# Setting one PSUM bank of the mixer apart, feeding transposes a pair earlier at the layer boundaries, and pumping the adaLN vectors at 1.25 in the first FFN

## The chip, the cores and the metric

The kernel runs on one core of a Trainium2 chip. Its time is the device time of one execution in microseconds; the change is judged by that time. The core's engines have a queue each: PE (matmul), DVE and ACT (elementwise work), POOL, and SP, which here issues most DMAs. An engine takes its instructions in order, so an instruction that waits holds up all behind it on that engine. [...]

## The reference, cut to what matters

One layer on 256 tokens of width 2048, in float32: a first FFN, a mixer, a second FFN, each with a layer norm whose shift, scale and gate come from a vector c (adaLN), and a scaled residual.

```python
mod = silu(c) @ w_ada + b_ada              # 9 vectors of 2048: shift, scale, gate for each of 3 parts
x = ln(ALPHA * x + gate0 * swiglu(modulate(x, ...), ffn1_w_in, ffn1_w_out))     # D_FF = 5632
m = modulate(x, ...) @ w_in                # queries, keys, values and gates of the mixer
#   8 softmax heads of width 128 with a forget-gate bias on the logits,
#   4 mLSTM heads (keys 128, values 256) behind a causal convolution of width 4
x = ln(ALPHA * x + gate1 * (concat(fox, mlstm) @ w_out))
x = ln(ALPHA * x + gate2 * swiglu(modulate(x, ...), ffn2_w_in, ffn2_w_out))
```

An mLSTM head forms, over all 256 tokens at once, a matrix of decays from its gates times the scores k.q, multiplies it with the values, and divides by a normaliser.

## The kernel before

**Products.** Every weight is streamed once from memory in pieces of 1 MB (`raw_...`, three buffers, issued on SP). A piece is split into a rounded part `hi` on ACT (L142) and the rest `lo` on DVE (L143), and each product is three matmuls: hi*hi (L369), lo*hi (L370), hi*lo (L371), in `mm3`. The tokens sit in PE's weight side or its moving side, with outputs of 128x256 or 128x512. Stages follow each other in time: first FFN in (tiles `s`, `gu_f`), its out projection (`o_f`), boundary 1, the mixer's input products (`mo`, `fv`, `mv`, `m0`, `m1`, `fb`, `fbk`, `fa`, `fak`, `b_fv`), its out projection (`o_mx`), boundary 2, second FFN.

**The adaLN queue.** The 9 vectors are not matmuls: DVE accumulates 128x1024 pieces of `w_ada` (`ar`, two buffers, 512 KB each) with `acc = ar * csil[k] + acc` (L157), 16 pieces per accumulator. Then `acc` is split into `ahi` and `alo`, PE sums over partitions with a matmul against ones (`bc`, L170), and DVE takes the diagonal of it (`dg` L188, reduce L190) or adds it to the gate (L211). All this is one generator; a stage calls `pump(rate)` after each of its weight pieces, which adds the rate to what is owed and runs that many accumulations. A `PAUSE` inside the generator ends a pump early, so that matmuls lie between the split, the sum and the diagonal. The rates stand in one line (`R_F, R_IN, R_OUT, R_MX, R_A, R_B`). `need(n)` runs the queue on until n parts are done, where the next stage uses them.

**PSUM.** Five banks (tag `mm`, `mm_tile`) rotate for the accumulating products, three (tag `aux`, `aux_tile`) for all else: transposes `tp`, `bc`, and in the mixer an mLSTM head's gate sums `gb`, scores `sps` and outputs `nps`. A tile of a tag takes the bank of the tile that many allocations before it and waits for that one's last reader.

**mLSTM heads.** `mlstm_head(o, h)` puts its gate sum (L1225) and scores (L1227) on PE, ACT turns the gate sum into decays (L1230, L1231), DVE masks them (L1232) and multiplies them with the scores (`dm`, L1233), PE forms `nps` (L1239, L1241), DVE the normaliser `dn`, ACT scales (L1248) and squares in place (L1249). The heads are side steps, taken between the weight pieces of `fb`, `fbk` and `fa`. The scores have two tiles: `sps` for 256 queries, and a corner of `gb`. The softmax heads' queries and keys (`pr_fb`, `pr_fbk`, `pr_fa`, `pr_fak`) are two tiles each, from `form_a_four`, read by ACT (L1307, L1312).

**Boundary.** `boundary` normalises 256 tokens, modulates and transposes them. For each pair of 128 columns and each half of the tokens, ACT forms `n` (L312), PE transposes it (`tp`, L316), DVE or ACT applies shift and scale (`xf`, L323 and L326), then `xhi_mx` (L332) and `xlo_mx` (L334) are split off. DVE's order (and ACT's, in the first part) is written out by hand with `next()` on the generators of `modulate_tile`; the first weight pieces' products run between. Boundary 1 has 8 such pairs, boundary 2 has 4. Elsewhere a scheduler sets each engine's order ahead of the run.

Of the kernel before, what the change touches and what calls it, by code (L numbers as in the profile page):

```python
# [14 lines left out]
P = 128  # L15
T = 256
# [16 lines left out]
def layer_kernel(  # L33
# [24 lines left out]
    wp.tile([P, 1024], F32R, tag="lo", bufs=6, name="lo_place")  # L58
    ap = ctx.enter_context(tc.tile_pool(name="ap", bufs=1))
    sm = ctx.enter_context(tc.tile_pool(name="sm", bufs=2))  # L60
    pm = ctx.enter_context(tc.tile_pool(name="pm", bufs=5, space=PSUM))
    pa = ctx.enter_context(tc.tile_pool(name="pa", bufs=3, space=PSUM))

    def mm_tile(name):
        return pm.tile([P, 512], F32, tag="mm", name=name)

    def aux_tile(name):
        return pa.tile([P, 512], F32, tag="aux", name=name)
# [204 lines left out]
    def ntag():  # L273
        seq[0] += 1
        return str(seq[0])
# [29 lines left out]
    def modulate_tile(v, a, k0, nk, rs, xT, xs=None, on_v=False):  # L305
        ts_ = slice(a * P, (a + 1) * P)
        n = npool.tile([P, nk * P], F32, tag="n", bufs=2, name=f"n_{ntag()}")
        r = res[:, a, k0 * P:(k0 + nk) * P]
        if on_v:
            V.tensor_scalar(out=n, in0=r, scalar1=rs[:, 2:3], scalar2=rs[:, 0:1], op0=ALU.add, op1=ALU.mult)  # L310
        else:
            S.activation(n, r, AF.Identity, bias=rs[:, 1:2], scale=rs[:, 0:1])  # L312
        tp = aux_tile(f"tp{ntag()}")
        tpv = tp.rearrange("p (k t) -> p k t", k=4)
        for q in range(nk):
            PE.transpose(tpv[:, q, :], n[:, q * P:(q + 1) * P], ident)  # L316
        yield
        xf = npool.tile([P, nk, P], F32, tag="xf" if xs is None else "xe", bufs=2 if xs is None else 6,
                        name=f"xf{ntag()}")
        for q in range(nk):  # L320
            k = k0 + q
            if q % 2 and (a or k0 >= 6):
                V.tensor_scalar(out=xf[:, q, :], in0=tpv[:, q, :], scalar1=scsh[:, v + 1, k:k + 1],  # L323
                                scalar2=scsh[:, v, k:k + 1], op0=ALU.mult, op1=ALU.add)
            else:
                S.activation(xf[:, q, :], tpv[:, q, :], AF.Identity,  # L326
                             bias=scsh[:, v, k:k + 1], scale=scsh[:, v + 1, k:k + 1])
            if xs is not None:
                xs[a, k] = xf[:, q, :]
        yield  # L330
        hi, lo = (x[:, k0:k0 + nk, ts_] for x in xT)
        S.copy(hi, xf)  # L332
        yield
        yield V.tensor_tensor(out=lo, in0=xf, in1=hi.bitcast(F32), op=ALU.subtract)  # L334
# [195 lines left out]
    def boundary(add_up, st, lgb, v, tag, xT, entry, nk, raws):  # L530
        mv, rs, sums, mr = ([small(n, t, f"{t}_{tag}{a}") for a in range(2)]
                            for n, t in ((2, "mv"), (1, "rs"), (10, "sums"), (3, "mr")))
        xs = {}
        ws = []
        sq = mm_tile(f"sq_{tag}")

        def w_hi():
            k = len(ws)
            hi = wp.tile([P, 1024], F32R, tag="hi", bufs=6, name=f"hi_{tag}e{k}")
            S.copy(hi, raws[k // 2][:, k % 2, :])  # L540
            ws.append((k, hi, wp.tile([P, 1024], F32R, tag="lo", bufs=6, name=f"lo_{tag}e{k}")))

        def w_lo(k):
            V.tensor_tensor(out=ws[k][2], in0=raws[k // 2][:, k % 2, :], in1=ws[k][1].bitcast(F32), op=ALU.subtract)

        dve, act = mybir.EngineType.DVE, mybir.EngineType.Activation
        m = [[modulate_tile(v, a, k, 2, mr[a], xT, xs if k < 6 else None, a + k == 0) for k in range(0, nk, 2)]
             for a in range(2)]
        m0, m1 = m
        with tc.manual_schedule(engines={dve, act}):  # L550
            for _ in add_up(0):
                pass
            together(row_std(mv[0], rs[0], st[0]))
            aff = [ln_affine(a, rs[a], mv[a], lgb, sums[a], sq) for a in range(2)]
            lns = [ln_stats(mr[a], sums[a]) for a in range(2)]
            w_hi()
            for _ in aff[0]:
                pass
            together(lns[0])
            up = add_up(1)  # L560
            together(lns[0])
            w_hi()
            next(m0[0])
            together(lns[0])
            next(m0[1])
# [24 lines left out]
            next(m1[1])  # L590
            next(m1[0])
            w_lo(1)
            next(m1[1])
            next(m1[0])
            next(m1[1])
            next(m1[0])
            w_lo(2)
            next(m1[1])
            w_lo(3)
        with tc.manual_schedule(engines={dve}):  # L600
            for i in range(3, len(m0)):
                for _ in range(2):
                    for b in (m0[i], m1[i]):
                        next(b)
                if i == 3:
                    next(m1[2])
                    for b in (m0[2], m1[2]):
                        next(b)
                for b in (m0[i], m1[i]):
                    next(entry, None)  # L610
                    next(b)
                    last = next(b)
        return last, mr, xs, ws
# [61 lines left out]

    R_F, R_IN, R_OUT, R_MX, R_A, R_B = 1.25, 1.2, 1, 1.42, 1.05, .6
    NP = 2
    right = dict(side="right")  # L680
    def at(rate):
# [314 lines left out]
    emptied = [None]  # L996


    def cols_form_b(c0, col, ws, use, name):
        ps = {(a, b): mm_tile(f"b_{name}{col}{a}{b}") for b in range(len(ws)) for a in range(2)}  # L1000
        cb = [sum(ws[:b]) for b in range(len(ws) + 1)]
        for u in range(4):
            for k4, hi, lo in load_w(W[u * 512:(u + 1) * 512, c0 + col:c0 + col + cb[-1]], 4, cb[-1],
# [29 lines left out]


    def form_a_four(c0, name, before_last=lambda: None):
        ps = [mm_tile(f"pr_{name}{i}") for i in range(2)]
        for u in range(4):
            if u == 3:
                before_last()
# [177 lines left out]
    def mlstm_head(o, h):  # L1217
# [2 lines left out]
            yield True  # L1220
        qm, km = o[:, 0, :], o[:, 1, :]
        gb = aux_tile(f"gb{h}")
        sps = [aux_tile(f"sps{h}")[:, :T], gb[:, T:T + P]]
        dm = mx.tile([P, T + P], F32, tag="dm", bufs=2, name=f"dm{h}")
        PE.matmul(gb[:, :T], sel(h), ng, start=True, stop=True)  # L1225
        for i in range(2):
# [103 lines left out]
    fox_heads(4, "b", lambda h: [f"o{h - 4}"])  # L1330
    side += [mlstm_out(h) for h in range(NMH)]
    fox_heads(0, "a", lambda h: [f"qs{h + 4}"])
    cols_form_b(C_FV, 0, [512], use_fv, "fv")
    done.add("fv0")
    xp.release()

# [175 lines left out]
```

## Time and profile before

| | |
|---|---|
| median of 3 runs | 1930.44 us (1929.65 to 1933.3) |
| profiled execution | 1936.89 us, of which the profile's span is 1935.1 |
| granted TensorE clock, mean | 0.994 |
| PE busy | 1892.8 us, 98% |
| DVE, ACT busy | 1486.0 us (77%), 952.6 us (49%) |
| DMA | 510.90 MB, mean 264 GB/s |

Where PE is busy nearly all the time, the time is its busy time plus its gaps; a row of waits names the engine and instruction that ended a gap. In timelines the bracket behind an instruction is the idle time just before it and its releaser. A clock below 1.00 stretches every matmul in that stretch.

### The profile page before, as it was taken

To read this page: it belongs to the slowest core of one execution; us is meant where nothing else is said; L and a number is where in the kernel's file an instruction comes from. 1 tells how busy PE (TensorE), PEld (TensorE's weight loads), DVE (VectorE), ACT (ScalarE), POOL (GpSimd) and SP (SyncE) were. 2 spreads that over 40 slices of the span, in tenths; PEclk is the share of its full clock that TensorE was granted. 3 is DMA by queue.
4 is the path that set the end of the run, shared out by engine and by line. 5 is a ranking of instruction groups with operands and counts; after the bars stand their busy time and mean duration, and the time that the engine had idled before them with its cause. 6 is when DMAs were issued, how large, how long until landed. Compare 5 with 4: busy or idle time off the path is not lost.

```text
span 1935.1 us, 32288 instructions
## 1 busy us (share of the span) xinstructions
PE 1892.8 (98%) x13085; PEld 1722.3 (89%) x13085; DVE 1486.0 (77%) x1838; ACT 952.6 (49%) x1359; POOL 56.4 (3%) x82
## 2 busy tenths in 40 slices
PE   6999999999999999999989999999999999999997
PEld 3999999999988887699989876999999999988886
DVE  6788988777788998888887888767766665555776
ACT  3554454443454554845755635555444444444552
POOL 1111100000000000100000000000000000000000
PEclk9999999999999999999999999999999999999998
DMA  9978969999898886498887895987776776755552
GB/s 354 377 260 315 326 224 302 308 313 320 292 331 289 287 303 218 154 326 295 300 290 237 301 301 167 314 298 240 253 254 225 262 237 196 238 187 187 194 196 87
DMA packets 283421, 510.90 MB, mean 264 GB/s; under 512 B 10850, under 2 KB 134146, under 8 KB 282248
## 3 DMA queue, kind: packets, MB, share of 16 engines
q1 hardware_dynamic: 275496, 480.53, 73.4%
q0 software_dynamic: 7776, 28.32, 4.2%
q8 instruction: 102, 1.67, 0.4%
q14 instruction: 47, 0.39, 0.1%
HBM read 506.71 MB, written 2.10 MB: 263 GB/s over the span
## 4 chain that ended last, share of the span: by engine, by line
PE 73%; issue 12%; DMA 7%; DVE 6%; ACT 1%; POOL 0%; SPq 0%; DVEq 0%; POOLq 0%; ACTq 0%
PE gu_f L370 8%; PE gu_f L371 8%; PE gu_f L369 8%; PE o_f L369 7%; PE o_f L371 7%; PE o_f L370 7%; DMA ar<-in_w_ada_dram 5%; PE s L369 5%; PE s L370 5%; PE s L371 5%; DVE acc L157 2%; PE fh L369 2%; PE fh L371 2%; PE fh L370 1%; PE fs L371 1%
## 5 line engine op out<-in xcount | busy, mean ns | idle before, releaser
L157 DVE SCALAR_TENSOR_TENSOR acc<-ar,csil,acc 128x1024 f32<-128x1024 f32 x242 | 307.7, 1272 | 91.6 <-DMA ar<-in_w_ada_dram 89.7
L370 PE MATMUL s<-xlo_f,hi_s 128*128 128x256 f32 x768 | 213.5, 278 | 1.8 <-DVE xlo_f L300 1.8
L369 PE MATMUL s<-xhi_f,hi_s 128*128 128x256 f32 x768 | 213.4, 279 | 0.0
L371 PE MATMUL s<-xhi_f,lo_s 128*128 128x256 f32 x768 | 213.2, 278 | 0.0
L371 PE MATMUL gu_f<-xhi_f,lo_f2i 128*128 128x256 f32 x768 | 212.0, 276 | 0.0
L369 PE MATMUL gu_f<-xhi_f,hi_f2i 128*128 128x256 f32 x768 | 212.0, 276 | 0.0
L370 PE MATMUL gu_f<-xlo_f,hi_f2i 128*128 128x256 f32 x768 | 212.0, 276 | 0.0
L143 DVE TENSOR_TENSOR lo_f2i<-raw_f2i,hi_f2i 128x1024 fp32r<-128x1024 f32 x96 | 117.6, 1225 | 89.0 <-ACT hi_f2i L142 89.0
L371 PE MATMUL gu_f<-xhi_f,lo_f1i 128*128 128x256 f32 x640 | 176.7, 276 | 0.0
L369 PE MATMUL gu_f<-xhi_f,hi_f1i 128*128 128x256 f32 x640 | 176.7, 276 | 0.0
L370 PE MATMUL gu_f<-xlo_f,hi_f1i 128*128 128x256 f32 x640 | 176.7, 276 | 0.0
L142 ACT CAST hi_f2i<-raw_f2i 128x1024 fp32r<-128x1024 f32 x96 | 100.7, 1049 | 135.2 <-PE gu_f L370 122.4
L142 ACT CAST hi_s<-raw_s 128x1024 fp32r<-128x1024 f32 x96 | 100.6, 1051 | 130.4 <-PE s L370 90.5
L370 PEld LDWEIGHTS s<-xlo_f,hi_s 128*128 128x128 f32 x768 | 145.3, 189 | 2.1 <-DVE xlo_f L300 2.1
L371 PEld LDWEIGHTS s<-xhi_f,lo_s 128*128 128x128 f32 x768 | 145.3, 189 | 0.0
L369 PEld LDWEIGHTS s<-xhi_f,hi_s 128*128 128x128 f32 x768 | 144.8, 189 | 0.2 <-ACT hT1b L827 0.2
L369 PEld LDWEIGHTS gu_f<-xhi_f,hi_f2i 128*128 128x128 f32 x768 | 144.2, 188 | 0.2
L370 PEld LDWEIGHTS gu_f<-xlo_f,hi_f2i 128*128 128x128 f32 x768 | 144.2, 188 | 0.2
L371 PEld LDWEIGHTS gu_f<-xhi_f,lo_f2i 128*128 128x128 f32 x768 | 144.2, 188 | 0.0
L143 DVE TENSOR_TENSOR lo_f2o<-raw_f2o,hi_f2o 128x1024 fp32r<-128x1024 f32 x88 | 107.7, 1224 | 44.9 <-ACT hi_f2o L142 44.8
L143 DVE TENSOR_TENSOR lo_s<-raw_s,hi_s 128x1024 fp32r<-128x1024 f32 x96 | 115.8, 1220 | 30.5 <-ACT hi_s L142 29.6
L369 PE MATMUL o_f<-hi_f2o,hh 128*128 128x512 f32 x344 | 135.2, 393 | 0.0
(449 smaller groups left out, 5377.1 us busy)
## 6 DMA issues: line engine op xcount, KB each, us to landing
ar<-in_w_ada_dram SPq DMA_DIRECT2D x227, 512.0 KB, 5.4
raw_f2i<-in_ffn_w_in_dram SPq DMA_DIRECT2D x48, 1024.0 KB, 5.2
raw_s<-in_ffn_w_in_dram SPq DMA_DIRECT2D x47, 1024.0 KB, 7.7
raw_f1o<-in_ffn_w_out_dram SPq DMA_DIRECT2D x44, 1024.0 KB, 7.5
raw_f2o<-in_ffn_w_out_dram SPq DMA_DIRECT2D x44, 1024.0 KB, 5.1
raw_f1i<-in_ffn_w_in_dram SPq DMA_DIRECT2D x40, 1024.0 KB, 6.9
ar<-in_w_ada_dram POOLq DMA_DIRECT2D x48, 512.0 KB, 6.9
raw_mxo<-in_w_out_dram SPq DMA_DIRECT2D x16, 1024.0 KB, 7.7
```

The costliest lines, as they stand in the source:

```text
L142: S.copy(hi, src)
L143: return V.tensor_tensor(out=lo, in0=src, in1=hi.bitcast(F32), op=ALU.subtract)
L157: V.scalar_tensor_tensor(out=acc, in0=raw, scalar=csil[:, k:k + 1], in1=acc, op0=ALU.mult, op1=ALU.add)
L369: PE.matmul(o, ah, bh, start=start, stop=False)
L370: PE.matmul(o, ah, bl, start=False, stop=False)
L371: PE.matmul(o, al, bh, start=False, stop=stop)
```

## The change

Three things. The five rotating banks become four with tag `mm` and one with tag `m5`; `mm_tile` counts turns and gives every fifth tile to `m5`, so that outside the mixer the turn is as before. In the mixer `form_a_four` and the last `cols_form_b` take only the four (`four=True`), and the fifth holds the scores `sps` of the mLSTM heads, which leave the three auxiliary banks. At the boundaries `columns(i + 1)` (the `n`, transposes and `xf` of the next pair) is called ahead of the lower parts of pair i, and the buffers of `xf` are 4 and 4 instead of 2 and 6. In the first FFN's input the rate goes from 1.2 to 1.25 accumulations per weight piece, of which 40 pump.

```diff
@@ -58,11 +58,19 @@
     wp.tile([P, 1024], F32R, tag="lo", bufs=6, name="lo_place")
     ap = ctx.enter_context(tc.tile_pool(name="ap", bufs=1))
     sm = ctx.enter_context(tc.tile_pool(name="sm", bufs=2))
-    pm = ctx.enter_context(tc.tile_pool(name="pm", bufs=5, space=PSUM))
+    pm = ctx.enter_context(tc.tile_pool(name="pm", bufs=1, space=PSUM))
     pa = ctx.enter_context(tc.tile_pool(name="pa", bufs=3, space=PSUM))
 
-    def mm_tile(name):
-        return pm.tile([P, 512], F32, tag="mm", name=name)
+    turn = [0]
+
+    def fifth_tile(name):
+        return pm.tile([P, 512], F32, tag="m5", name=name)
+
+    def mm_tile(name, four=False):
+        turn[0] = 0 if four else turn[0] % 5 + 1
+        if turn[0] == 5:
+            return fifth_tile(name)
+        return pm.tile([P, 512], F32, tag="mm", bufs=4, name=name)
 
     def aux_tile(name):
         return pa.tile([P, 512], F32, tag="aux", name=name)
@@ -315,8 +323,7 @@
         for q in range(nk):
             PE.transpose(tpv[:, q, :], n[:, q * P:(q + 1) * P], ident)
         yield
-        xf = npool.tile([P, nk, P], F32, tag="xf" if xs is None else "xe", bufs=2 if xs is None else 6,
-                        name=f"xf{ntag()}")
+        xf = npool.tile([P, nk, P], F32, tag="xf" if xs is None else "xe", bufs=4, name=f"xf{ntag()}")
         for q in range(nk):
             k = k0 + q
             if q % 2 and (a or k0 >= 6):
@@ -544,8 +551,8 @@
             V.tensor_tensor(out=ws[k][2], in0=raws[k // 2][:, k % 2, :], in1=ws[k][1].bitcast(F32), op=ALU.subtract)
 
         dve, act = mybir.EngineType.DVE, mybir.EngineType.Activation
-        m = [[modulate_tile(v, a, k, 2, mr[a], xT, xs if k < 6 else None, a + k == 0) for k in range(0, nk, 2)]
-             for a in range(2)]
+        m = [[modulate_tile(v, a, k, 2, mr[a], xT, xs if 4 * a <= k < 6 else None, a + k == 0)
+              for k in range(0, nk, 2)] for a in range(2)]
         m0, m1 = m
         with tc.manual_schedule(engines={dve, act}):
             for _ in add_up(0):
@@ -598,14 +605,19 @@
             next(m1[1])
             w_lo(3)
         with tc.manual_schedule(engines={dve}):
-            for i in range(3, len(m0)):
+            def columns(i):
                 for _ in range(2):
                     for b in (m0[i], m1[i]):
                         next(b)
+
+            columns(3)
+            for i in range(3, len(m0)):
                 if i == 3:
                     next(m1[2])
                     for b in (m0[2], m1[2]):
                         next(b)
+                if i + 1 < len(m0):
+                    columns(i + 1)
                 for b in (m0[i], m1[i]):
                     next(entry, None)
                     next(b)
@@ -675,7 +687,7 @@
 
 
 
-    R_F, R_IN, R_OUT, R_MX, R_A, R_B = 1.25, 1.2, 1, 1.42, 1.05, .6
+    R_F, R_IN, R_OUT, R_MX, R_A, R_B = 1.25, 1.25, 1, 1.42, 1.05, .6
     NP = 2
     right = dict(side="right")
     def at(rate):
@@ -996,8 +1008,8 @@
     emptied = [None]
 
 
-    def cols_form_b(c0, col, ws, use, name):
-        ps = {(a, b): mm_tile(f"b_{name}{col}{a}{b}") for b in range(len(ws)) for a in range(2)}
+    def cols_form_b(c0, col, ws, use, name, four=False):
+        ps = {(a, b): mm_tile(f"b_{name}{col}{a}{b}", four) for b in range(len(ws)) for a in range(2)}
         cb = [sum(ws[:b]) for b in range(len(ws) + 1)]
         for u in range(4):
             for k4, hi, lo in load_w(W[u * 512:(u + 1) * 512, c0 + col:c0 + col + cb[-1]], 4, cb[-1],
@@ -1033,7 +1045,7 @@
 
 
     def form_a_four(c0, name, before_last=lambda: None):
-        ps = [mm_tile(f"pr_{name}{i}") for i in range(2)]
+        ps = [mm_tile(f"pr_{name}{i}", True) for i in range(2)]
         for u in range(4):
             if u == 3:
                 before_last()
@@ -1220,7 +1232,7 @@
             yield True
         qm, km = o[:, 0, :], o[:, 1, :]
         gb = aux_tile(f"gb{h}")
-        sps = [aux_tile(f"sps{h}")[:, :T], gb[:, T:T + P]]
+        sps = [fifth_tile(f"sps{h}")[:, :T], gb[:, T:T + P]]
         dm = mx.tile([P, T + P], F32, tag="dm", bufs=2, name=f"dm{h}")
         PE.matmul(gb[:, :T], sel(h), ng, start=True, stop=True)
         for i in range(2):
@@ -1330,7 +1342,7 @@
     fox_heads(4, "b", lambda h: [f"o{h - 4}"])
     side += [mlstm_out(h) for h in range(NMH)]
     fox_heads(0, "a", lambda h: [f"qs{h + 4}"])
-    cols_form_b(C_FV, 0, [512], use_fv, "fv")
+    cols_form_b(C_FV, 0, [512], use_fv, "fv", True)
     done.add("fv0")
     xp.release()
```

The number of instructions of each engine stays the same; their order changes. Line numbers after the change are larger by 7 to 12.

PE, in the mixer, around mLSTM head 2 (`nps_10508` is head 0's second output, `gb_10524` and `sps_10525` head 2's gate sum and scores), before:

```order
L1239 MATMUL nps_10508<-yM_8718,dm_10332 128x257
L1241 MATMUL nps_10508<-yM_8718,dm_10332 128x257
L1225 MATMUL gb_10524<-ng,rowsel 128x256
L1227 MATMUL gb_10524<-o_9834 128x128
L369 MATMUL pr_fbk_10444<-xhi_mx,hi_fbk_10540 128x256
L370 MATMUL pr_fbk_10444<-xlo_mx,hi_fbk_10540 128x256
...
L1227 MATMUL sps_10525<-o_9834 128x256
```

The same place after (`nps_10523`, `gb_10539`, `sps_10540`):

```order
L1251 MATMUL nps_10523<-yM_8733,dm_10372 128x257
L1253 MATMUL nps_10523<-yM_8733,dm_10372 128x257
L1237 MATMUL gb_10539<-ng,rowsel 128x256
L1239 MATMUL sps_10540<-o_9847 128x256
L1239 MATMUL gb_10539<-o_9847 128x128
L376 MATMUL pr_fbk_10459<-xhi_mx,hi_fbk_10555 128x256
```

The scores move from 22 rows behind the gate sum to the row next to it.

DVE, in the mixer, up to the multiplication of head 0's decays with its scores (`dm_10332`), before:

```order
L143 TENSOR_TENSOR lo_fbk_10541<-raw_fbk_10538,hi_fbk_10540 128x1024
L157 SCALAR_TENSOR_TENSOR acc_0_10402<-ar_0_2_10409,csil,acc_0_10402 128x1024
L188 TENSOR_TENSOR dg_1_1_10316<-bc_1_1_10313,ident 128x512
L157 SCALAR_TENSOR_TENSOR acc_0_10402<-ar_0_3_10412,csil,acc_0_10402 128x1024
L190 TENSOR_REDUCE scsh<-dg_1_1_10316 128x4
L1232 TENSOR_TENSOR dm_10332<-dm_10332,trir 128x128
L192 TENSOR_TENSOR scsh<-scsh,bcol 128x2x4
L1232 TENSOR_TENSOR dm_10332<-dm_10332,trir 128x128
L1233 TENSOR_TENSOR dm_10332<-sps_10331,dm_10332 128x256
L1233 TENSOR_TENSOR dm_10332<-gb_10330,dm_10332 128x128
```

DVE after, from the same multiplication (`dm_10372`) to that of head 1 (`dm_10447`, whose last part reads `gb_10445`):

```order
L1245 TENSOR_TENSOR dm_10372<-sps_10371,dm_10372 128x256
L165 SCALAR_TENSOR_TENSOR acc_0_10120<-ar_0_10_10285,csil,acc_0_10120 128x1024
L1245 TENSOR_TENSOR dm_10372<-gb_10370,dm_10372 128x128
L151 TENSOR_TENSOR lo_fbk_10638<-raw_fbk_10635,hi_fbk_10637 128x1024
L151 TENSOR_TENSOR lo_fbk_10666<-raw_fbk_10635,hi_fbk_10665 128x1024
L165 SCALAR_TENSOR_TENSOR acc_0_10120<-ar_0_11_10354,csil,acc_0_10120 128x1024
L1244 TENSOR_TENSOR dm_10447<-dm_10447,trir 128x128
L165 SCALAR_TENSOR_TENSOR acc_0_10120<-ar_0_12_10357,csil,acc_0_10120 128x1024
L1245 TENSOR_TENSOR dm_10447<-sps_10446,dm_10447 128x256
L1244 TENSOR_TENSOR dm_10447<-dm_10447,trir 128x128
L151 TENSOR_TENSOR lo_fbk_10736<-raw_fbk_10733,hi_fbk_10735 128x1024
L1245 TENSOR_TENSOR dm_10447<-gb_10445,dm_10447 128x128
```

The diagonal of `bc_1_1` and its reduce no longer stand ahead of head 0's masks; three lo products and two accumulations stand between head 0's last part and that of head 1.

DVE, in the mixer's out projection, at the last accumulations of part 2 (`ar_2_14`, `ar_2_15`), before:

```order
L438 SCALAR_TENSOR_TENSOR res<-res,o_mx_11741 128x512
L143 TENSOR_TENSOR lo_mxo_30_12319<-raw_mxo_3_12316,hi_mxo_30_12318 128x1024
L157 SCALAR_TENSOR_TENSOR acc_2_12026<-ar_2_14_12257,csil,acc_2_12026 128x1024
L441 BN_STATS st_mx_11737<-res 128x6
L157 SCALAR_TENSOR_TENSOR acc_2_12026<-ar_2_15_12296,csil,acc_2_12026 128x1024
L143 TENSOR_TENSOR lo_mxo_31_12323<-raw_mxo_3_12316,hi_mxo_31_12322 128x1024
L436 TENSOR_TENSOR o_mx_12138<-o_mx_12138,gate 128x512
L143 TENSOR_TENSOR lo_mxo_10_12331<-raw_mxo_1_12328,hi_mxo_10_12330 128x1024
```

And after:

```order
L448 BN_STATS st_mx_11752<-res 128x6
L165 SCALAR_TENSOR_TENSOR acc_2_11906<-ar_2_15_12150,csil,acc_2_11906 128x1024
L445 SCALAR_TENSOR_TENSOR res<-res,o_mx_11755 128x512
L151 TENSOR_TENSOR lo_mxo_10_12234<-raw_mxo_1_12231,hi_mxo_10_12233 128x1024
L151 TENSOR_TENSOR alo_2_0_12192<-acc_2_11906,ahi_2_0_12191 128x512
...
L445 SCALAR_TENSOR_TENSOR res<-res,o_mx_11757 128x512
L151 TENSOR_TENSOR lo_mxo_30_12333<-raw_mxo_3_12330,hi_mxo_30_12332 128x1024
L448 BN_STATS st_mx_11753<-res 128x6
L151 TENSOR_TENSOR lo_mxo_31_12337<-raw_mxo_3_12330,hi_mxo_31_12336 128x1024
L196 TENSOR_TENSOR dg_2_0_12270<-bc_2_0_12267,ident 128x512
```

The last accumulation, `ar_2_15`, moves from two rows ahead of the add-up of the second 1024 columns to the add-up of the first; the first half of its split (`alo_2_0`) and its diagonal (`dg_2_0`) stand among the lo products instead.

## The prediction

> **What bounds the kernel now.** I read the page first, then the waits of PE, then busy time by stage, and last the timeline around each wait.
>
> ```profile
> span 1935.1 us, 32288 instructions
> ...
> PE 1892.8 (98%) x13085; PEld 1722.3 (89%) x13085; DVE 1486.0 (77%) x1838; ACT 952.6 (49%) x1359; POOL 56.4 (3%) x82
> ```
> ```profile
> PE sps L1227 <- DVE dm L1233: 5.8, 2, 4.4
> ...
> PE o_mx L370 <- DVE lo_mxo L143: 1.8, 2, 1.1
> PE bc L170 <- DVE alo L143: 1.4, 1, 1.4
> ...
> PE o_mx L369 <- DVE res L438: 1.1, 1, 1.1
> PE tp L316 <- DVE xf L323: 0.7, 1, 0.7
> ...
> PE o_mx L369 <- ACT yF L1054: 0.5, 1, 0.5
> ...
> PE nps L1239 <- DVE dm L1233: 0.2, 1, 0.2
> PE sps L1227 <- ACT nps L1249: 0.2, 1, 0.2
> ```
>
> PE is busy 98% of the span, and neither the number of its instructions nor that of any other engine changes. So the change can only win or lose what PE waits. These rows (us in total, times, longest) are all of PE's waits that lie in stages the change touches: 5.8 + 1.8 + 1.4 + 1.1 + 0.7 + 0.5 + 0.2 + 0.2 = 11.7 us. The next fence has busy time by stage (length, then PE, PEld, DVE, ACT, POOL, the granted PE clock, DMA share, GB/s).
>
> ```profile
> 276.00:516.00 240.00, 240.00 (x2107) 239.48 (x2105) 192.94 (x206) 104.10 (x126) 0.56 (x1) 1.00 0.92 307
> ...
> 1210.00:1500.00 290.00, 289.92 (x2414) 283.55 (x2413) 209.67 (x245) 144.86 (x206) 0.00 (x0) 1.00 0.80 264
> 1500.00:1780.00 280.00, 280.00 (x2026) 261.83 (x2025) 162.94 (x160) 124.93 (x145) 0.00 (x0) 1.00 0.67 219
> ```
> ```profile
> 983.00:987.00 4.00, 0.07 (x1) 0.00 (x0) 3.38 (x11) 0.56 (x2) 0.00 (x0) 0.90 0.84 270
> 987.00:993.00 6.00, 5.54 (x24) 5.39 (x25) 4.33 (x5) 2.50 (x7) 0.00 (x0) 0.50 1.00 346
> 993.00:1000.00 7.00, 7.00 (x57) 6.83 (x57) 5.36 (x10) 3.70 (x8) 0.00 (x0) 1.00 0.58 193
> ```
>
> In the first FFN's input stage (276 to 516) and in the whole second FFN PE never stands still: a faster pump there earns nothing by itself. The last three rows show a cost that the list of waits leaves out. PE stood still from 983 to 987; then 24 matmuls took 6.00 us at clock 0.50, where 57 took 7.00 us at clock 1.00, so 24 would take 2.95: 3.05 us more. The mixer's heads thus cost 5.8 + 0.2 + 0.2 + 3.05 = 9.2 us.
>
> **Heads (fifth bank).** Rows of PE, ACT and DVE around heads 1 and 2 (start, duration, engine, line; idle time and its releaser in brackets):
>
> ```profile
> 972.11 0.70 PE L1227 MATMUL sps<-o 128*128 128x256 f32 x2 [1.36 <-DVE dm L1233]
> 979.94 0.48 PE L1225 MATMUL gb<-ng,rowsel 128*128 128x256 f32 x1
> 987.46 1.19 PE L1227 MATMUL sps<-o 128*128 128x256 f32 x2 [4.39 <-DVE dm L1233]
> ```
> ```profile
> 975.72 1.05 ACT L142 CAST hi_fbk<-raw_fbk 128x1024 fp32r<-128x1024 f32 x1 [1.15 <-PE pr_fbk L370]
> 987.17 0.39 ACT L1249 ACTIVATE nps<-yM 128x256 f32<-128x256 f32 x1
> ```
> ```profile
> 968.64 0.68 DVE L188 TENSOR_TENSOR dg<-bc,ident 128x512 f32<-128x512 f32 x1
> ...
> 971.97 0.28 DVE L1233 TENSOR_TENSOR dm<-gb,dm 128x128 f32<-128x128 f32 x1
> ...
> 979.21 1.22 DVE L143 TENSOR_TENSOR lo_fbk<-raw_fbk,hi_fbk 128x1024 fp32r<-128x1024 f32 x1
> ...
> 981.88 1.28 DVE L157 SCALAR_TENSOR_TENSOR acc<-ar,csil,acc 128x1024 f32<-128x1024 f32 x1 [1.45 <-DMA ar<-in_w_ada_dram]
> ```
>
> `sps2` at 987.46 is put down to DVE's `dm`, but no `dm` ends there on DVE. What ends at 987.46 is ACT's square of `nps00` (987.17): `sps2` takes the auxiliary bank that `nps00` holds. With a bank of its own `sps2` no longer waits for it: 4.39 goes, and 0.19 at `sps3`. `sps1` now waits for head 0's `dm<-sps`, on the same DVE as before, but the order after has `dg` and its reduce (I take 0.6 us each, the row's 0.68 less the overlap of neighbours) no longer ahead of it: 1.36 shrinks to about 0.2.
>
> What is late next? The auxiliary banks now turn gb0, gb1, nps00, nps01, gb2: `gb2` takes `gb1`'s bank and waits for DVE's `dm<-gb1`, which the order puts behind three lo products and two accumulations. `gb2` would be due at 979.94 - 1.4 = 978.5. On DVE head 0's `dm` ends near 971.1, one accumulation and its last part by 972.4, a lo product by 973.6; the next lo needs the cast of 975.72, which PE releases 1.2 us earlier, so it runs from 975.6 to 976.8; two accumulations (2.4), the masks and `dm<-sps1` (0.8), one lo product (1.15) and `dm<-gb1` (0.28) end at 981.4. `gb2` waits 2.9 us (0 if the scheduler's order is met, 4.5 if one accumulation finds its row as late as at 981.88). With 0.3 for later squares the heads keep 0.2 + 2.9 + 0.3 = 3.4, and gain 5.8, provided that the clock stays up. A wait of 1.36 kept it; in the row of 983 to 987 the mean of 0.90 over 4 us means 0.8 us at half clock, so it fell about 3.1 us into the wait. 2.9 is just below, and I take the full clock; the half clock would give 3.05 back.
>
> [...]
>
> **Boundaries.** In boundary 1 the n, transposes and `xf` of pair i+1 now stand ahead of hi/lo of pair i; boundary 2 has four pairs and one turn of that loop, so nothing moves there.
>
> ```profile
> 803.67 0.44 PE L316 MATMUL tp<-ident,n 128*128 128x128 f32 x2 [0.73 <-DVE xf L323]
> ```
> ```profile
> 798.60 1.05 ACT L142 CAST hi_mo<-raw_mo 128x1024 fp32r<-128x1024 f32 x1 [1.48 <-DMA raw_mo<-in_w_in_dram]
> 801.96 0.59 ACT L312 ACTIVATE n<-res,mr 128x256 f32<-128x256 f32 x1
> ```
>
> The transposes that waited 0.73 move seven matmuls earlier on PE, but their `n` still stands on ACT behind two casts, the first of which waits 1.48 for its weights; `n` ends at about 802.1 and PE arrives at about 801.1. The stall changes its place and its releaser: 0, between -0.7 (the whole stall) and +1.
>
> **R_IN and the queue behind it.** 40 pumps at 1.25 make 50 accumulations in the first FFN's input instead of 48. They hide: the row of 276 to 516 has DVE free for 47 us and DMA for 8%, that is 19 us, and two accumulations take 2.5 us of DVE. From there the queue runs 2 to 8 accumulations ahead, so other pieces of it meet the places where PE waits.
>
> ```profile
> 755.16 0.50 PE L170 MATMUL bc<-ahi,trir 128*128 128x512 f32 x1
> 760.04 0.50 PE L170 MATMUL bc<-alo,trir 128*128 128x512 f32 x1 [1.40 <-DVE alo L143]
> ```
> ```profile
> 759.30 0.68 DVE L143 TENSOR_TENSOR alo<-acc,ahi 128x512 fp32r<-128x512 f32 x1
> ```
>
> Here the order after has `alo` six lo products of 1.15 us earlier on DVE, done near 753, and PE takes both halves together where it took the first, near 755: -1.4 (0 if DVE ran 2 us late).
>
> ```profile
> 1088.33 1.21 DVE L143 TENSOR_TENSOR lo_mxo<-raw_mxo,hi_mxo 128x1024 fp32r<-128x1024 f32 x1
> ...
> 1120.26 2.60 DVE L157 SCALAR_TENSOR_TENSOR acc<-ar,csil,acc 128x1024 f32<-128x1024 f32 x2 [1.85 <-DMA ar<-in_w_ada_dram]
> ...
> 1127.67 1.28 DVE L157 SCALAR_TENSOR_TENSOR acc<-ar,csil,acc 128x1024 f32<-128x1024 f32 x1 [1.94 <-DMA ar<-in_w_ada_dram]
> ...
> 1134.78 1.28 DVE L157 SCALAR_TENSOR_TENSOR acc<-ar,csil,acc 128x1024 f32<-128x1024 f32 x1 [1.76 <-DMA ar<-in_w_ada_dram]
> ...
> 1139.45 1.29 DVE L436 TENSOR_TENSOR o_mx<-o_mx,gate 128x512 f32<-128x512 f32 x2
> ...
> 1164.29 1.28 DVE L157 SCALAR_TENSOR_TENSOR acc<-ar,csil,acc 128x1024 f32<-128x1024 f32 x1 [1.35 <-DMA ar<-in_w_ada_dram]
> ```
> ```profile
> 1168.55 0.50 PE L370 MATMUL o_mx<-lo_mxo,yh 128*128 128x512 f32 x1 [1.07 <-DVE lo_mxo L143]
> ```
>
> In the mixer's out projection the last accumulations of part 2, with the wait of 1.35 at 1164.29, stood just ahead of the lo products that PE waited for (1.07 of them at 1168.55). After, the last one is before them by ten rows; two `alo`, a `dg` and a reduce of 0.6 each come instead. The waits list's 1.8 us go (0 to 2.3). The price is paid earlier: between the lo product at 1088.33 and the first add-up at 1139.45 stand 16 accumulations instead of 12. With two row buffers they come in pairs every 7.1 to 7.4 us (1120.26, 1127.67, 1134.78), 3.6 us each: 14 beyond the two already loaded take 50 us, which is about the stretch's own length (51). So the wait of 1.1 at the first add-up stays and grows by an estimated 1.0 (-1.1 to +5). At the stage's start DVE has fewer accumulations before the softmax, ACT's copy of `b_fv` comes earlier and the 0.5 goes (+1.4 if the four-bank turn makes another tile wait for the same copies).
>
> **The four-bank turn.** Only `pr_fa1` gets a bank that may still be read: `pr_fb1`'s, which ACT reads last for head 7.
>
> ```profile
> 1008.50 0.28 PE L369 MATMUL pr_fa<-xhi_mx,hi_fa 128*128 128x256 f32 x1
> ```
> ```profile
> 1003.78 0.38 ACT L1307 ACTIVATE qs<-pr_fb 128x256 f32<-128x256 f32 x1
> ```
>
> 4.3 us lie between; ACT's order after puts a scaling and a square (1 us) ahead of that read: hidden, 0, with 3.3 us to spare. If they are used up, the wait is what is left over. [...]
>
> **Sum.** -5.8 (heads) - 1.4 (`bc`) + 0 (boundary) - 0.5 + 1.0 - 1.8 (out projection) = -8.5 us. The profiled execution took 1936.89 (1935.1 of span, 1.8 around it), 6.5 above the median; none of the terms hangs on that difference, so it is carried over: 1928.4 against that execution, 1930.44 - 8.5 = 1921.9 against the median.
>
> **The rivals.**
> - Half clock after `gb2`: DVE is slightly later than worked out, the wait passes 3.1 us. For: DVE's accumulations there waited 1.45 for rows. Price 3.05: 1925.0. Chance 0.20.
> - The wait only moves: `gb2` takes over all but about 2.5 of the heads' 9.2, and the out projection's tail is paid back at the first add-up (+1.8): 1930.44 - 2.5 - 1.4 + 1.3 = 1927.8. Chance 0.10.
> - Every wait goes: 9.2 + 1.4 + 0.7 + 0.5 + 1.1 + 1.8 = 14.7, 1915.7. Against: `dm<-gb1` stands late in the order. Chance 0.08.
> - Four banks are too few: if ACT's reads came 8 us later than now, `pr_fa1` would wait 8 - 3.3 = 4.7 us, and an `o_mx` tile the 1.4 + 0.5 worked out above: 1921.9 + 6.6 = 1928.5. It decides from 3.3 us of lateness. Against: the 4.3 us at `pr_fa1`, and ACT's share of 49%. Chance 0.05.
> - Slower: the out projection starves. The 16 accumulations wait for rows on DVE, the lo products queue behind them, PE behind those. At 3.6 us each it is just even; every 0.1 us more costs 1.4 us. At 4.2 the gain is gone, at 4.5 (12.6 later) the time is 1934.5, and slower by more than 0.2% from there on. For: DMA waits in each pair above. Against: they arise between rows that DVE frees late, and the SP queue has room. Chance 0.12, 1936 as its middle.
>
> **How the numbers follow.** The forecast has 0.45: 1921.9, its own range 1918 to 1925 from the bounds of `gb2` and of the add-up. A measurement of this kernel can tell about 0.2%, 3.9 us, from no change: 1926.6 to 1934.3 counts as the same. Faster: 0.45 + 0.20 + 0.08 = 0.73, less 0.01 for upper ends; same: 0.10 + 0.05 + 0.01; slower: 0.12. The range from 1915.0 to 1931.0 leaves out the slower rival and the far end of all waits gone.
>
> **What would show it.** Right: no wait of `sps` beyond 0.5 us; `gb2` waiting 2 to 3.3 us for `dm` at clock 1.00; no wait of `bc` on `alo`; none of `o_mx` on `lo_mxo` after the first add-up. Wrong: `gb2` at half clock, PE waits of over 2 us for `lo_mxo` or `res` between 1085 and 1140, a wait of `pr_fa`, or any PE wait in either FFN.

## The result

| | before | after |
|---|---|---|
| median of the runs taken together | 1932.48 us (1929.65 to 1933.42, 6) | 1945.94 us (1942.38 to 1949.98, 6) |
| ratio, 95% interval | | 1.0066, 1.0053 to 1.0079 |
| profiled execution | 1936.89 us | 1942.38 us |

The change makes the kernel slower by 0.66%, 12.8 us of 1932.48 (the two medians lie 13.5 apart; three of the six runs of before are those of the table ahead of the prediction). The forecast was 1921.9 and its range ended at 1931.0, so it is wrong in sign and in range. The two profiled executions lie only 5.5 us apart: that of before is above the median of its kernel, that of after is the quickest of its six.

The page of after, span and busy time by engine:

```profile
span 1940.7 us, 32286 instructions
...
PE 1894.7 (98%) x13085; PEld 1724.8 (89%) x13085; DVE 1484.6 (76%) x1838; ACT 952.5 (49%) x1359; POOL 57.4 (3%) x82
```

The work is the same, so the difference is waiting. PE's waits in after (us in total, times, longest), those of the stages that the change touches:

```profile
PE sps L1239 <- ACT qs L1319: 3.3, 1, 3.3
PE fh L376 <- ACT hi_fh L150: 3.0, 1, 3.0
...
PE tp L324 <- ACT n L320: 1.6, 3, 1.0
...
PE fh L378 <- DVE lo_fh L151: 1.5, 2, 0.8
PE pr_fb L378 <- DVE lo_fb L151: 1.3, 2, 0.8
PE fs L376 <- ACT hi_fs L150: 1.3, 1, 1.3
...
PE o_f L377 <- DVE lo_f1o L151: 1.2, 2, 1.1
PE b_mv L377 <- DVE lo_mv L151: 1.1, 1, 1.1
PE o_mx L376 <- DVE res L445: 0.9, 1, 0.9
PE fs L378 <- DVE lo_fs L151: 0.8, 1, 0.8
```

Gone, as forecast, are `bc` on `alo`, `o_mx` on `lo_mxo` and on `yF`. New are `fh` and `fs`, the tiles with which the second FFN begins, where before PE did not wait at all, `pr_fb` and `b_mv` in the mixer's input products, and `o_f` in the first FFN's out projection. Cutting PE's record at the first matmul of each stage gives the sizes (us; the other stages differ by at most 1.0):

| stage | before | after | difference |
|---|---|---|---|
| `b_mv` to `pr_fb` | 91.8 | 94.3 | +2.5 |
| `pr_fb` to `pr_fa` (heads) | 61.6 | 58.3 | -3.3 |
| `o_mx` to `fh` (out projection, boundary 2) | 127.7 | 124.2 | -3.5 |
| `fh` to `fs` | 101.9 | 109.3 | +7.4 |
| `fs` to `gu_f` | 99.5 | 102.8 | +3.3 |

The first part of the second FFN, `fh` and `fs`, takes 10.7 us longer: 6.6 are the waits listed above (3.0 + 1.5 + 1.3 + 0.8), and two stretches of 3.4 us at half clock, from 1255.3 and 1323.6 on, cost 3.4 more. The queue of SP shows why PE waits. Before (start, duration, engine and line, tile, count of DMAs):

```profile
1205.35 27.10 SPq L344 DMA_DIRECT2D raw_fh<-in_ffn_w_in_dram  x8
1232.75 2.70 SPq L179 DMA_DIRECT2D ar<-in_w_ada_dram  x2
1236.21 0.37 SPq L344 DMA_DIRECT2D raw_fh<-in_ffn_w_in_dram  x1
```

After:

```profile
1200.88 6.42 SPq L351 DMA_DIRECT2D raw_fh<-in_ffn_w_in_dram  x3
1213.07 1.69 SPq L187 DMA_DIRECT2D ar<-in_w_ada_dram  x2
1214.86 0.42 SPq L351 DMA_DIRECT2D raw_fh<-in_ffn_w_in_dram  x1
1218.16 3.21 SPq L187 DMA_DIRECT2D ar<-in_w_ada_dram  x2
1221.47 0.42 SPq L351 DMA_DIRECT2D raw_fh<-in_ffn_w_in_dram  x1
...
1240.66 2.70 SPq L187 DMA_DIRECT2D ar<-in_w_ada_dram  x2
1243.41 0.46 SPq L351 DMA_DIRECT2D raw_fh<-in_ffn_w_in_dram  x1
1246.20 3.47 SPq L187 DMA_DIRECT2D ar<-in_w_ada_dram  x2
1249.72 1.29 SPq L351 DMA_DIRECT2D raw_fh<-in_ffn_w_in_dram  x1
```

Before, eight weight pieces go out ahead of the first pair of `ar` rows; after, three. From there a pair stands ahead of every piece, and each pair waits until DVE has freed its two buffers. SP's own waits from 1150 to 1260 in after:

```profile
SPq L187 <- DVE acc L165: 20.6, 12, 2.3
```

So the pieces go out every (1249.72 - 1214.86) / 5 = 7.0 us. How fast PE uses them is in the stretch 1220 to 1240 of after (length, then PE, PEld, DVE, ACT, POOL, clock, DMA share, GB/s):

```profile
1220.00:1240.00 20.00, 20.00 (x179) 20.00 (x178) 14.55 (x13) 7.96 (x14) 0.00 (x0) 1.00 0.98 319
```

A piece feeds 48 matmuls (768 of `fh` by 16 pieces): 48 x 20 / 179 = 5.4 us. PE starts `fh` at 1212.2, so piece 8 is due at 1212.2 + 7 x 5.4 = 1250; SP sent it at 1243.41. A piece needs 8.9 us to land there:

```profile
raw_fh<-in_ffn_w_in_dram SPq DMA_DIRECT2D x2, 1024.0 KB, 8.9
```

It lands at 1252.3, ACT splits it, and PE stands still:

```profile
1252.41 1.99 ACT L150 CAST hi_fh<-raw_fh 128x1024 fp32r<-128x1024 f32 x2 [7.74 <-DMA raw_fh<-in_ffn_w_in_dram]
```
```profile
1253.51 0.38 PE L376 MATMUL fh<-xhi_f,hi_fh 128*128 128x256 f32 x1 [2.96 <-ACT hi_fh L150]
...
1254.77 0.39 PE L378 MATMUL fh<-xhi_f,lo_fh 128*128 128x256 f32 x1 [0.76 <-DVE lo_fh L151]
```

Before, pairs came too, and nearly as slowly, a piece every 6.6 us from 1236.21 to 1269.15, but piece 9 (1236.21), the first behind a pair, was due at 1216.2 + 8 x 5.5 = 1260: 24 us of spare, which the pairs did not use up before the stage ended. After, piece 4 starts with 1228.4 - 1214.86 = 13.5 and each later one has 1.6 less.

Where the pairs come from stands in `pump`: `owed` grows by the rate at every call, and a `PAUSE` ends the call without reducing it. Two accumulators of the queue matter here, of 16 rows each, both for the vectors of the second FFN: `ar_2_...`, here called part 2, and the one behind it, here called part 6, the sixth part that the queue is given. The pauses of part 2 leave accumulations owed. Before, they fall to boundary 2 and the start of `fh` (`alo` at 1211.58, the `dg` at 1228.72 and 1239.92), and no `ar` row is asked for there. With the faster pump they begin in the out projection (`alo` at 1143.65 and 1159.53, a `dg` at 1156.15), part 6 starts early in `fh`, and what is owed is paid there two at a time.

### The profile page after: what moved, and what is told of

Its sections match the earlier page's. It is cut to its first block, busy times and chain, and to the rows that moved or that the text cites. A ratio compares the mean times of both kernels' runs of the same rounds, so it can differ in the third digit from the quotient of the medians.

```text
span 1940.7 us, 32286 instructions
## 1 busy us (share of the span) xinstructions
PE 1894.7 (98%) x13085; PEld 1724.8 (89%) x13085; DVE 1484.6 (76%) x1838; ACT 952.5 (49%) x1359; POOL 57.4 (3%) x82
## 4 chain that ended last, share of the span: by engine, by line
PE 78%; DMA 10%; DVE 7%; issue 3%; ACT 1%; POOL 0%; SPq 0%; DVEq 0%; ACTq 0%; POOLq 0%
PE gu_f L378 8%; PE gu_f L376 8%; PE gu_f L377 8%; PE o_f L376 8%; PE o_f L378 8%; PE o_f L377 8%; DMA ar<-in_w_ada_dram 6%; PE s L376 4%; PE s L378 4%; PE s L377 4%; DVE acc L165 2%; DMA raw_fh<-in_ffn_w_in_dram 2%; PE fs L378 2%; PE fs L376 1%; PE fs L377 1%
```

## The experiments

The theory: the rate of 1.25 alone makes the loss, by pairs of `ar` rows ahead of the weight pieces of `fh` and `fs`. The rivals: the banks or the boundary make it; the early start of part 6 harms, whatever its pace; only SP's order is the carrier, or only DVE's extra accumulations; the DMA moves no more. Edits are against after unless it says "before". Intervals are 95%.

**e1, the rate put back.**

```diff
-    R_F, R_IN, R_OUT, R_MX, R_A, R_B = 1.25, 1.25, 1, 1.42, 1.05, .6
+    R_F, R_IN, R_OUT, R_MX, R_A, R_B = 1.25, 1.2, 1, 1.42, 1.05, .6
```

> Banks and boundary as changed, the rate back at 1.2. SP's order in the second FFN is again that of before: eight pieces raw_fh in a row ahead of the first pair of ar. Theory (the rate shifts the adaLN queue, and on SP its loads hold the next raw_fh): no waits of fh or fs, heads as in the prediction or better, 1921 to 1927 us. Rival (the banks or the boundary cost the time): at or above 1940.

1935.82 us against 1935.33, 0.9998 (0.9986 to 1.0011). The loss is gone, but the banks and the boundary gain nothing either: both sides missed.

**e2, the rate alone** (before with the rate of after).

```diff
-    R_F, R_IN, R_OUT, R_MX, R_A, R_B = 1.25, 1.2, 1, 1.42, 1.05, .6
+    R_F, R_IN, R_OUT, R_MX, R_A, R_B = 1.25, 1.25, 1, 1.42, 1.05, .6
```

> Only the rate, 1.25 in place of 1.2; banks and boundary as before. SP's order in the second FFN is that of the change: three raw_fh, then pairs of ar between single raw_fh. Theory: the same waits of fh and fs as with the whole change, about 10 us with the half clock, and the heads' waits of before in addition: 1945 to 1955 us. Rival: 1930 to 1934.

1954.64, 1.0104 (1.0086 to 1.0122), within the theory's range. The rate alone costs 1%. PE's waits in it:

```profile
PE fh L369 <- ACT hi_fh L142: 3.0, 2, 2.3
...
PE fs L369 <- ACT hi_fs L142: 2.2, 1, 2.2
```

`fh` to `fs` takes 110.6 us, `fs` to `gu_f` 101.2, and `b_mv` to `pr_fb` 99.1 instead of 91.8.

**e3, the banks alone** (before with `fifth_tile`, the new `mm_tile`, `four=True` and the scores' bank, all as in after).

```diff
-        sps = [aux_tile(f"sps{h}")[:, :T], gb[:, T:T + P]]
+        sps = [fifth_tile(f"sps{h}")[:, :T], gb[:, T:T + P]]
```

> Only the banks. Theory: the wait of 4.4 us at sps2 goes and the half clock with it; gb2 keeps a wait of 0 to 3 us; 1923 to 1928 us. Rival (four banks too few): 1930 or more, with waits at pr_fa or o_mx.

1934.57, 0.9993 (0.9984 to 1.0003). No gain: the time is the rival's. Of its waits `pr_fa` has none, and that of `o_mx` for `yF` comes with the old banks too, 1.9 us in e4. The waits of `sps` are gone, and that of `lps` for DVE's `s` is new:

```profile
PE lps L1100 <- DVE s L1105: 2.2, 1, 2.2
PE o_mx L377 <- ACT yF L1062: 2.0, 1, 2.0
...
PE nps L1247 <- DVE dm L1241: 0.5, 1, 0.5
```

**e4, the boundary alone** (before with `columns` and the `xf` buffers).

```diff
+                if i + 1 < len(m0):
+                    columns(i + 1)
                 for b in (m0[i], m1[i]):
```

> Only the order at the boundary. Theory: the stall of 0.7 us moves to another transpose and another releaser, within 1.5 us of before: 1930 to 1934 us. Rival (the earlier transposes make DVE or ACT late): 1936 or more.

1934.46, 1.0000 (0.9989 to 1.0011). As the forecast had it: the wait changes its releaser, and no time.

**e5, the early features without accumulations.**

```diff
     xT = new_xT("f2")
+    owed[0] = 0
...
-        cols_1024(raws, xs, ws, guw, gu_load, gups, xT, at(R_A), 0, 4)
+        cols_1024(raws, xs, ws, guw, gu_load, gups, xT, at(0), 0, 4)
...
-                        f"{tag}{j}_{gu}", at(R_B if kh else R_A), (kh,))
+                        f"{tag}{j}_{gu}", at(R_B if kh else 2.1 * (j >= 4)), (kh,))
```

> The whole change, but the adaLN queue is held from the end of the mixer to the sixth piece pair of the second FFN and then runs at 2.1 per piece: SP's order is nine raw_fh in a row, then pairs of ar between single raw_fh, as in before. Theory (the pairs of ar on SP, come too early, hold raw_fh back): the waits of fh and fs and their half clock go, about 9 us less than the whole change, so 2 to 8 us above before. Rival (the loss is DVE's load or DMA's bandwidth over the whole stage, whatever the order): still 11 or more above before.

1936.36, 1.0010 (1.0000 to 1.0020), as the theory had it. Nine pieces now go out first, and PE does not wait from 1195 to 1420:

```profile
1202.23 30.04 SPq L351 DMA_DIRECT2D raw_fh<-in_ffn_w_in_dram  x9
1232.57 1.69 SPq L187 DMA_DIRECT2D ar<-in_w_ada_dram  x2
```

**e6, the rows on another queue.** From the second FFN's first piece on, POOL issues `ar` instead of SP (in both loops that load rows).

```diff
-                SP.dma_start(raw, src[k * P:(k + 1) * P])
+                (G_ if late[0] else SP).dma_start(raw, src[k * P:(k + 1) * P])
...
     xT = new_xT("f2")
+    late[0] = True
```

> The whole change, with the same accumulations in the same places of DVE, but from boundary 2 on the loads of ar are issued by POOL instead of SP, so SP has only weight pieces. Theory (in-order SP): fh and fs wait no more, 2 to 8 us above before. Rival 1 (DVE's load): fh keeps waiting for lo_fh. Rival 2 (bandwidth): raw_fh lands as late as before, fh waits for hi_fh as with the whole change.

1952.70, 1.0084 (1.0068 to 1.0099): as slow as after; `fh` to `gu_f` takes 217.1 us in its profile, 212.1 in after. SP's order by itself is not the carrier. No `fh` waits for `hi_fh` any more, and it is DVE that stands in front of a pair; the lower part of the piece is queued behind it, and PE behind that (DVE, then PE):

```profile
1273.15 1.28 DVE L165 SCALAR_TENSOR_TENSOR acc<-ar,csil,acc 128x1024 f32<-128x1024 f32 x1 [2.87 <-DMA ar<-in_w_ada_dram]
1274.35 2.35 DVE L151 TENSOR_TENSOR lo_fh<-raw_fh,hi_fh 128x1024 fp32r<-128x1024 f32 x2
```
```profile
1275.63 0.39 PE L379 MATMUL fh<-xhi_f,lo_fh 128*128 128x256 f32 x1 [3.68 <-DVE lo_fh L151]
```

**e7, an early start without the debt** (before, four steps of the queue taken at boundary 2, so that part 6 starts behind three pieces).

```diff
     xT = new_xT("f2")
+    for _ in range(4):
+        next(ada_left["g"])
     raws = [gu_raw(u) for u in range(3)]
```

> The kernel before, with the four pauses of part 2 run off just ahead of boundary 2, so that the loads of ar begin after three raw_fh as with the change; rate, banks and first boundary are those of before. Single loads of ar stand between raw_fh after the first two pairs, so the hold is about half as strong. Theory: waits of fh appear, 2 to 8 us above before. Rival (needs the whole shift of the queue, from the first FFN on): within 2 us of before.

1935.40, 0.9998 (0.9989 to 1.0008). The early start costs nothing: after two pairs the rows come singly. So it is not the start that harms, it is the pace.

**e8, the last tile in the old turn** (e1, and this).

```diff
-    cols_form_b(C_FV, 0, [512], use_fv, "fv", True)
+    cols_form_b(C_FV, 0, [512], use_fv, "fv")
```

> Banks and boundary with the rate at 1.2, and the last value tiles b_fv back in the turn of five, so that only one tile of the out projection takes a bank that their copies to yF still read. All engines' orders are those of the rate-back run. Theory: the wait of 1.4 to 2.0 us of o_mx for yF, and the half clock that one profile showed there, shrink: 1 to 3 us below the rate-back run, up to 3 below before. Rival (the copy is late for the last tile too): the same as the rate-back run.

1936.42, 1.0007 (0.9996 to 1.0017). No gain: a miss. In its profile the wait for `yF` is down to 0.2 us, but `o_mx` waits 2.1 for `lo_mxo`.

**e9, the debt struck out.** One line:

```diff
     xT = new_xT("f2")
+    owed[0] = 0
     raws = [gu_raw(u) for u in range(3)]
```

> The whole change, with what the pump owes set to zero at boundary 2: the accumulations of part 6 begin after three raw_fh as with the change, but after the first pair one ar, not two, stands between one raw_fh and the next. Theory (a pair of rows per piece takes 7 us round its two buffers where PE needs 5.5 for a piece; one row fits): fh and fs wait no more, 1 to 5 us above before. Rival (an early start alone is the harm): as the whole change, 11 or more above before.

1935.80, 1.0005 (0.9994 to 1.0016). Part 6 starts as early as in after, behind three pieces, but its rows come singly after the first pair:

```profile
1217.52 1.69 SPq L187 DMA_DIRECT2D ar<-in_w_ada_dram  x2
1219.30 0.42 SPq L351 DMA_DIRECT2D raw_fh<-in_ffn_w_in_dram  x1
1223.57 0.37 SPq L187 DMA_DIRECT2D ar<-in_w_ada_dram  x1
1224.03 0.43 SPq L351 DMA_DIRECT2D raw_fh<-in_ffn_w_in_dram  x1
```

Piece 4 to piece 8 go out at 1219.30 and 1237.48, 4.5 us apart where PE needs 5.4, and PE has no wait from 1195 to 1420. `fh` to `fs` is 100.9, `fs` to `gu_f` 99.5. It also answers the rival that the DMA moves no more: from 1220 to 1256 e9 moves 343 GB/s, after only 304. But a pair with every piece at PE's pace, 2.1 MB in 5.4 us, would take 388 GB/s (an estimate), more than any stretch shown here moves (376 at most); whether the DMA would bind next was not tested.

**e10, a third row buffer** in `fh` and `fs`.

```diff
-                raw = ap.tile([P, 2, 512], F32, tag="araw", bufs=2, name=f"ar{v}_{j}_{k}")
+                where, tag, n = (third[0], "aw", 1) if third[0] and k % 3 == 2 else (ap, "araw", 2)
+                raw = where.tile([P, 2, 512], F32, tag=tag, bufs=n, name=f"ar{v}_{j}_{k}")
```

> The whole change, with a third row buffer for ar while the second FFN's features run; the scheduler then puts three ar between raw_fh pieces, for fewer pieces. Theory (the turn of the two buffers sets the pace): fh waits less, 2 to 8 us above before. Rival (the number of accumulations between two lo products of raw_fh decides, whatever the buffers): fh waits as much or more, 11 or more above before.

1949.22, 1.0057 (1.0039 to 1.0074). No cure. Its profiled execution took 3872.75 us, twice the others, so none of its lines is read, and whether the buffers' turn, DVE or the DMA held it stays open.

**e11, the accumulations without their rows.** In part 6, which is `(6, 3)` in the code, only rows 0 and 8 of 16 are loaded; all 16 accumulations run, on old data, so that scale and shift of 512 columns are not those of the reference.

```diff
             for k in range(KD):
-                raw = ap.tile([P, 2, 512], F32, tag="araw", bufs=2, name=f"ar{v}_{j}_{k}")
-                SP.dma_start(raw, src[k * P:(k + 1) * P])
+                if (v, j) != (6, 3) or k % 8 == 0:
+                    raw = ap.tile([P, 2, 512], F32, tag="araw", bufs=2, name=f"ar{v}_{j}_{k}")
+                    SP.dma_start(raw, src[k * P:(k + 1) * P])
                 ada_acc(acc, raw, k)
```

> The whole change, but the last accumulator of the vectors for the second FFN loads only two of its sixteen rows and adds these eight times each; its 16 DVE instructions stay, 14 loads of 512 KB are left out, so shift and scale of 512 columns are wrong. Theory (the rows' loads are waited for, by SP ahead of raw_fh and by DVE ahead of the lo products): fh does not wait, 1 to 5 us above before. Rival (DVE's work on the accumulations itself): fh waits for lo_fh, 8 or more above before.

1944.77, 1.0041 (1.0028 to 1.0054): more than expected. Where the rows are left out the waits go, from 4.5 to 0.8 us:

```profile
PE fs L377 <- ACT hi_fs L150: 1.7, 1, 1.7
...
PE fh L379 <- DVE lo_fh L151: 0.8, 1, 0.8
PE fs L379 <- DVE lo_fs L151: 0.8, 1, 0.8
```

So it is the rows that `fh` waits for, not DVE's work on them. `fs` keeps its wait, for the rows of the next part. Its median is 9.4 above that of before; against the profile of before, `fh` to `gu_f` holds 5.3 of it (103.9 and 102.8), and `b_mv` to `pr_fb`, where the rows are all loaded, 4.2 (96.0).

**e12 to e15, single profiles of before, e1, e3 and e1 again**, on one chip, on where the gain of the banks went.

> The kernel before, profiled once more, no edit. If the heads' stretch is typical: 57 to 62 us from the first pr_fb to the first pr_fa, out projection's start without a wait of over 1 us. If the first profile was an accident: below 55.

> The rate-back kernel (banks and boundary as changed, rate 1.2), profiled once more, no edit. If the heads' gain is real and lost elsewhere: again 51 to 54 us in the heads' stretch, and 3 us or more over before between pr_fa and fh or in an earlier stage. If one profile was an accident: the heads' stretch is 56 or more.

> The banks-only kernel, profiled once more, no edit. The same two readings as for the rate-back kernel: heads' stretch 51 to 54 with a loss elsewhere, or 56 or more.

> The rate-back kernel, profiled a third time, no edit; the same two readings.

1932.78, 1940.04, 1938.13 and 1936.07, beside 1931.52 for before. With the profiles above this makes two groups at the rate of 1.2 (us, the runs in order; in both rows no run of one group lies within the other):

| stretch | five banks (before, e12, e4, e7) | four and one (e1, e13, e15, e3, e14, e8) |
|---|---|---|
| `pr_fb` to `pr_fa` | 61.6, 55.2, 57.3, 60.6 | 51.7, 54.0, 52.0, 52.5, 53.6, 53.7 |
| `pr_fa` to `o_mx` | 80.0 in all | 82.1, 84.7, 86.1, 82.7, 85.4, 84.5 |

The means are 58.7 against 52.9 and 80.0 against 84.3: the heads gain 5.8 us, and the next stretch gives back 4.3. What stands in it, in the second profile of e3 (e14):

```profile
1023.71 0.49 PE L1100 MATMUL lps<-qs 128*128 128x128 f32 x2 [2.18 <-DVE s L1105]
```

PE comes earlier to the softmax heads and its `lps` waits for DVE's `s` there: 1.8 to 2.2 us in all six, and at most 0.2 with the five banks; in e15 some of the `pr_fa` matmuls then run at half clock, the longest in 415 ns where the median is 276 (the same form takes 0.41 us in after at 1324.06, at clock 0.50; e3's longest `pr_fa` takes 284). The means of the next stretches take back the 1.5 that remain, though there the groups overlap: `o_mx` to `fh` 127.9 against 128.6, `fh` to `fs` 101.8 against 103.0.

## Why the prediction was wrong

**The step that failed** is the one behind the rate: that in the first FFN's input stage and in the whole second FFN "PE never stands still: a faster pump there earns nothing by itself", and "They hide". What was costed was the two more accumulations in the stage that makes them. What they shift was followed only to "the places where PE waits". It stood in the sum at nothing; in after it costs 10.7 us in the second FFN and 2.5 in the mixer's input products. The prediction's own last sign of being wrong, a PE wait in an FFN, came. In the second FFN PE waited nowhere, and that was read as room; what would have told is each weight piece's spare, the time from its issue to its use, against the 8.9 us of its landing. The order of SP's queue, eight pieces or three ahead of the first pair, can be seen without a run: the expectation of e1 states it. e2 (rate alone, +1.04%), e1 (rate back) and e9 (debt struck out) show it three ways.

**The slower rival** had the mechanism, accumulations that wait for rows with lower parts and PE queued behind, but put it in the mixer's out projection, at a chance of 0.12. There it did not come: `o_mx` waits 0.9 for `res` where it was to wait 2.1, and `o_mx` to `fh` takes 124.2 to 127.2 us in the six profiles at 1.25 (after, e2, e5, e6, e9, e11; mean 125.2) and 126.6 to 128.8 in the four of before's banks at 1.2 (before, e4, e7, e12; mean 127.9): 2.7 less, where the steps gave -0.5 + 1.0 - 1.8 = -1.3. The sign is right, the first add-up was sized too high. The rival's mechanism came earlier, in the mixer's input products (below).

**The heads** were sized at -5.8, and wrongly split. `sps1` was to wait 0.2 and `gb2` 2.9. In after (PE, then DVE):

```profile
977.78 0.67 PE L1239 MATMUL sps<-o 128*128 128x256 f32 x2 [3.26 <-ACT qs L1319]
```
```profile
974.49 1.27 DVE L165 SCALAR_TENSOR_TENSOR acc<-ar,csil,acc 128x1024 f32<-128x1024 f32 x1
975.68 1.22 DVE L151 TENSOR_TENSOR lo_fbk<-raw_fbk,hi_fbk 128x1024 fp32r<-128x1024 f32 x1
...
977.22 0.41 DVE L1245 TENSOR_TENSOR dm<-sps,dm 128x256 f32<-128x256 f32 x1
```

The fifth bank is a single buffer, and head 1's scores wait for head 0's `dm<-sps`, which ends at 977.63. (The row names ACT's `qs`, which ends at 977.70. But in all five profiles with this wait, after, e5, e6, e9 and e11, PE starts 0.15 us behind that `dm`, and 0.08 to 0.23 behind `qs`.) The forecast had that `dm` end near 971.1; DVE was busy without a gap from 971.02 with lower parts and accumulations, which its order puts ahead, so it came 6.5 us later. `gb2` did not wait. The half clock was to go; it comes, from 978.8 on.

This too is the rate's doing: with the same banks at 1.2 that `dm` ends at 971.17 in e1, and the `sps` waits add up to at most 0.9 us in each of the six profiles, where at 1.25 this one is 3.26 in all five. So at 1.25 the stretch takes 57.2 to 59.2 us, as much as the 58.7 mean of the five-bank profiles at 1.2 (the one profile with five banks at 1.25, e2, has 60.0). At 1.2 the banks do win 5.8 us in the stretch, and that this is the forecast's figure is luck: the route is another, and the 9.2 us that were there to win were partly those of one execution (two profiles of before give 61.6 and 55.2). **A second step failed** here, and the rate does not explain it: the sum let nothing behind the heads pay the gain back, and at 1.2 the next stretches do (e12 to e15).

**A second cost of the rate** was not in any step: `b_mv` to `pr_fb` takes 94.3 to 99.1 us in the six profiles at 1.25 and 91.8 to 92.4 in the ten at 1.2. In after it is the waits of `pr_fb` for `lo_fb` and of `b_mv` for `lo_mv`, 2.4 of the 2.5 us. Ahead of the `lo_mv` in question DVE's accumulation at 881.11 waited 3.31 us for its row (3.4 to 4.0 in e5, e9 and e11): the carrier that e6 showed. That e9 ends level with before fits this loss and the shorter out projection: against the means of the five-bank profiles at 1.2 it loses 5.2 us here, and wins 3.1 there and 0.9 in `fh` to `fs`.

**Right by the wait, and not by the time,** was `bc`. No profile at 1.25 has its wait near 760 us. But in five of the six the `bc` that now comes at 867 to 874 waits 0.5 to 2.2 us, and `o_f` waits 1.2 to 2.7 for `lo_f1o`, which it does in none of the ten at 1.2. So `o_f` to `mo`, where the 1.4 was to be won, takes 247.9 us in before and in after.

**Right** was the boundary: `tp` waits 0.95 for ACT's `n` at 802.53, where it had waited 0.73 for `xf`, and e4 measures 1.0000. The prediction's list of waits left out 0.6 us of `tp` for `n` (two waits of 0.3, one at each boundary), which it called complete; they are there in after too and change nothing.

## What to carry to other kernels

A queue that is shared out by a rate carries its debt along: follow a changed rate to every later stage, to where the debt is paid, and compare there the spare of each streamed piece (due time less issue time) with its landing time, above all where nothing waits yet. A stream with two small buffers can pace whatever is queued behind it, on the queue that issues it (after: a piece every 7.0 us where PE needs 5.4) and on the engine that consumes it (e6: PE waits 3.68 us for a lower part behind a row that DVE waited 2.87 for); one more buffer was no cure (e10: 1949.22). A wait that is taken away on one engine brings the others' lateness forward (of the heads' 5.8 us at 1.2 the next stretch takes 4.3): look for the next place where the faster engine meets the slower one.

## What the runs showed of the hardware

The forecast let the half clock begin 3.1 us into a wait. The runs show no such fixed length. The trace records the granted clock; these are stretches of after around three waits (length, PE, clock, DMA share, GB/s):

```profile
978.50:982.50 4.00, 4.00 (x23) 0.57 1.00 376
...
1255.00:1259.00 4.00, 4.00 (x23) 0.57 0.69 228
1320.00:1324.00 4.00, 1.91 (x12) 0.95 1.07 354
```

A mean of 0.57 over 4 us is 3.4 us at half clock, and these cost 1.7 us. In after the clock falls at 978.8, 1255.3 and 1323.6, each time with PE at work again: behind waits of 3.26 us (ended 977.78), of 2.96 and 0.76 (1253.51 and 1254.77), and of 1.33 and 0.76 (1321.55 and 1322.81). In e6 PE's matmuls slow from 0.28 to 0.42 us at 1276.4, behind a wait of 3.68 (ended 1275.63). In before the clock falls inside the wait of 4.39, 1.3 us ahead of its end. Of the waits ahead of 1323.6 none is longer than 1.33 us and both make 2.09, and the clock fell; behind e3's single wait of 2.19 for `s` (ended 1020.57) it stays at 1.00 to 1082. So the length alone does not tell: about 2 us of waiting was followed by 1.7 us of loss in after and by none in e3, and what decides was not shown. The 3.3 us at clock 1.00 among the prediction's signs are not borne out by after, where 3.26 was followed by the half clock.
